# Token mixer of a hybrid trunk: 23 weight pieces rounded by converting transfers, their rests made by an adding transfer

## The chip, the cores and the metric

The kernel runs on one core of one Trainium2 chip. The metric is the device time of one launch in microseconds (us), as the median over runs. Less is better.

## The reference

One layer of a decoder trunk on 16 meta tokens and 512 real tokens of width 1024, in float32: a SwiGLU feed-forward (FFN1), a token mixer, a second SwiGLU feed-forward (FFN2), each added to the residual.

```python
h = h + 0.5 * swiglu(rms_norm(h, g1), ffn1_w_in, ffn1_w_out)
h = h + token_mixer(rms_norm(h, gm), ...)
h = h + 0.5 * swiglu(rms_norm(h, g2), ffn2_w_in, ffn2_w_out)

def token_mixer(h, ...):
    proj = h @ w_in                    # 1024 x (3*512 + 8 + 512 + 2*128 + 2*1024)
    qa, ka, va, fa, qb, kb, vb, ga, gb = split(proj)
    # per-head rms_norm of qa, ka, qb, kb
    log_f = log_sigmoid(fa + forget_bias)
    o_fox = fox_attention(qa, ka, va, log_f)         # 8 heads, causal, with decay
    o_swa = swa_attention(qb, kb, vb, sinks, bias)   # window 128, meta keys, sinks
    y = sigmoid(ga) * (o_fox @ w_branch_fox) + sigmoid(gb) * (o_swa @ w_branch_swa)
    return y @ w_out
```

## The kernel before

**Split products.** TensorE multiplies fp32r numbers, which are rounded float32. To keep float32 accuracy each factor is split into a rounded part and a rest, `x = xH + xL`, `w = wH + wL`, and a product is three matmuls into one PSUM tile: `xH wH`, `xH wL`, `xL wH`. The helper `prod` records all of them, so they stand at L301, L302 and L304 wherever they are used. For the 16 meta tokens `tok_step` uses a packed tile `xm` and two matmuls, L1009 and L1010.

**Pieces of weights.** All weights come in pieces of up to 128 x 1024 float32 (512 KB), in the order of the list `pieces`. A piece of kind "w" goes through three tiles of the pool `wp`: `raw` (loaded by SP's queue, L252), `wh` (rounded by ScalarE, `hi`, L133) and `wl` = `raw - wh` (VectorE, `lo`, L140). Each name has three buffers that are used in turn. Other kinds ("A" to "D") belong to seven-product blocks in the FFNs; some of their loads are added onto a loaded tile by a transfer on POOL's queue (`add`, L211).

**Who drives them.** The user of a piece calls `piece()`. It splits pieces up to `state["ahead"]` = 3 from the one in use (`split_to`) and loads up to 5 from it (`load_to`). The call stands where the first matmul of the piece is recorded, so the loads and splits are recorded ahead of it; a scheduler then orders each engine's recorded instructions. Every engine works through its own order strictly.

**The mixer.** The projection of `w_in` runs in nine chunks of 256 columns, two pieces each: first the first half of `va` (with the 8 forget columns; the pieces are `w0`), then `ka` (k0), `qa` (q0), the other half of `va`, k1, q1, `kv` (keys and values of the window branch), qb0, qb1. Then three gate pieces `wg`, four pieces of the first branch matrix `wbr[0]`, the last gate, and the pieces of `wbr[1]`. Chunks that make tokens go by tiles of 128 tokens (`tok_chunk`), gates and branches by features (`feat_steps`). A chunk of k or q is followed by head norms (`head_norm`: sums of squares on ScalarE, L1061; the power of -1/2 on POOL, `rsq`, L351; scaling on VectorE, L1073), a transpose on TensorE and a split into `qH`, `qL` or `kH`, `kL`. Attention units (scores L1221, exponentials L1181, values L1281) are woven between the chunks.

**Around the start of the mixer** POOL also casts `xm` (L898, L899), loads four small tables (L967 to L970) and fills `v` and `qn` (L1100, L1126).

Of the kernel before, what the change touches and what calls it, by code (L numbers as in the profile page):

```python
# [11 lines left out]
F32 = mybir.dt.float32  # L12
F32R = mybir.dt.float32r
BF16 = mybir.dt.bfloat16
AF = mybir.ActivationFunctionType
ALU = mybir.AluOpType
# [4 lines left out]
P = 128  # L21
# [11 lines left out]
PW = 4 * 264  # L33
# [5 lines left out]
NG = 4  # L39
# [43 lines left out]
def kernel(  # L83
# [22 lines left out]
    V, A, G, PE, SP = nc.vector, nc.scalar, nc.gpsimd, nc.tensor, nc.sync  # L106

    cp = ctx.enter_context(tc.tile_pool(name="const", bufs=1))
    wp = ctx.enter_context(tc.tile_pool(name="wts", bufs=3))
# [6 lines left out]
    def nm(s):  # L116
        nid[0] += 1
        return f"{s}_{nid[0]}"
# [5 lines left out]
    def psum(whole=False):  # L124
        if banks["turn"] is not None:
            whole = banks["turn"] = not banks["turn"]
        tag = "pt" if whole else "ps"
        return pp.tile([P, 512], F32, tag=tag, name=nm(tag))

    def hi(o, i, scale=None):  # L130

        if scale is None:
            return A.copy(o, i)  # L133
        return A.activation(o, i, AF.Identity, scale=scale)
# [13 lines left out]
    pieces = []  # L148
# [26 lines left out]
    ffn_pieces(w1i, w1o, False)  # L175
    for c in (4, 2, 0, 5, 3, 1, 8, 6, 7):
        for k in (0, 4):
            pieces.append(("w", [(wm[c][:, k : k + 4, :], 4, 256)]))
            if c == 4:
                pieces[-1][1].append((wfa[:, k : k + 4, :], 4, 8))  # L180
    pieces += [("w", [(wg[m], 8, 128)]) for m in range(NG - 1)]
    pieces += [("w", [(wbr[0, c], 4, 256)]) for c in range(4)]
    pieces.append(("w", [(wg[NG - 1], 8, 128)]))
    pieces += [("w", [(wbr[1, c], 4, 256)]) for c in range(3)]

# [1 line left out]
    for step in GATES:  # L187
        if step[0] != "sliding":
            m = KD * step[0] + step[1]
# [8 lines left out]
    raws, split = {}, {}  # L198

    xm_place = lambda n: cp.tile([P, KD * P], F32R, tag="xm", name=nm(n))  # L200
    state = {"use": 0, "load": 0, "split": 0}
    shared = {}

    def land(tile_, ap):
# [8 lines left out]
    def load_first(b1, b2, n):  # L213

        raw = wp.tile([P, PW], F32, tag="raw", name=nm("raw"))
        land(raw, b1[:, :n])
        land(raw[:, 128 * n :], b2[:, :n])
        add(raw[:, 128 * n :], b2[:, n:])
        return raw[:, : 256 * n], 2 * n, 128

    def load_others(b1, b2, n):

        w = 128 * n
        fpool = shared["tp"]
        c = fpool.tile([P, PW], F32, tag="rawC", name=nm("rawC"), bufs=2)
        d = fpool.tile([P, 512], F32, tag="rawD", name=nm("rawD"), bufs=2)
        land(c, b1)
        add(c, b2[:, :n])
        land(d, b2[:, n:])

        def sums():
            t = fpool.tile([P, PW], F32, tag="tc", name=nm("tc"), bufs=1)
            V.tensor_tensor(out=t[:, :w], in0=c[:, :w], in1=d[:, :w], op=ALU.add)
            V.tensor_tensor(out=t[:, w : 2 * w], in0=t[:, :w], in1=c[:, w : 2 * w], op=ALU.add)  # L234
            return t[:, : 2 * w], 2 * n, 128

        return sums, (c[:, : 2 * w], 2 * n, 128), (d[:, :w], n, 128)

    def load_to(n):
        while state["load"] < min(n, holds[0] if holds else n, len(pieces)):  # L240
            c = state["load"]
            state["load"] += 1
            kind, *what = pieces[c]
            if kind == "w":
                parts = what[0]
                nk = parts[0][1]
                w = sum(p[2] for p in parts)
                raw = wp.tile([P, PW], F32, tag="raw", name=nm("raw"))
                rv = raw[:, : nk * w].rearrange("p (k c) -> p k c", c=w)
                c0 = 0  # L250
                for ap, _, n_ in parts:
                    SP.dma_start(rv[:, :, c0 : c0 + n_], ap)  # L252
                    c0 += n_
                raws[c] = (raw[:, : nk * w], nk, w)
            elif kind == "A":
                raws[c] = load_first(*what)
            elif kind == "B":
                raws[c], raws[c + 1], raws[c + 2] = load_others(*what)
# [5 lines left out]
    def split_to(n):  # L264
        while state["split"] < min(n, len(pieces)):
            c = state["split"]
            load_to(c + 1)
            state["split"] += 1
            raw = raws.pop(c)
            if callable(raw):  # L270
                with tc.issue_after(shared["lo"]):
                    raw = raw()
            raw, nk, w = raw
            if pieces[c][0] == "D":
                wd = shared["wd"]()
                wh, wl = wd[:, :512], wd[:, 512:1024]
            else:
                wh, wl = (wp.tile([P, PW], F32R, tag=t, name=nm(t)) for t in ("wh", "wl"))
            b = slice(0, nk * w)
            shared["split"] = hi(wh[:, b], raw[:, b]), lo(wl[:, b], raw[:, b], wh[:, b])  # L280
            shared["lo"] = getattr(shared["split"][1], "ins", shared["split"][1])
            split[c] = tuple(t[:, : nk * w].rearrange("p (k c) -> p k c", c=w) for t in (wh, wl))

    def piece(ahead=None, then=None):

        c = state["use"]
        state["use"] += 1
        if then is not None and c in split:
            then(split[c])
            then = None  # L290
        split_to(c + (ahead or state["ahead"]))
        load_to(c + 5)
        if then is not None:
            then(split[c])
        return split.pop(c)

    def prod(outs, sH, sL, first, last, more=False):

# [706 lines left out]
    def tok_step(ps, i, w, k, width):  # L1005
        c0, _ = ttile[i]
        wH, wL = w[k // 4]
        if i == 0:
            PE.matmul(ps[:, :width], xm[:, k], wH[:, k % 4], start=k == 0, stop=False)  # L1009
            PE.matmul(ps[:, :width], xm[:, k], wL[:, k % 4], start=False, stop=k == KD - 1)  # L1010
            return
        prod(
            [(ps[:, :width], wH[:, k % 4], wL[:, k % 4])],
            xH[:, k, c0 : c0 + P],
            xL[:, k, c0 : c0 + P],
            k == 0,
            k == KD - 1,
        )
# [10 lines left out]
    def tok_chunk(alloc, tiles, evac, finish=None):  # L1029

        w, box = [], {}

        def one(i, half):
            if not w:
                alloc()
                w.extend([piece(), piece()])
            if half == 0:
                box[i] = psum()
            for k in range(4 * half, 4 * half + 4):
                tok_step(box[i], i, w, k, 256)  # L1040
            if half:
                box[i] = evac(i, tok_result(box[i], i, 256))
                if i - 1 in box and box[i - 1] is not None:
                    box[i - 1]()

        def end():
            if box[tiles[-1]] is not None:
                box[tiles[-1]]()
            finish()

        st = [lambda i=i, h=h: one(i, h) for i in tiles for h in range(2)]
        if finish is not None:
            st.append(end)
        return st
# [42 lines left out]
    def v_tile():  # L1097

        v = new("v", [P, NB + 1, 512])
        G.memset(v[:, 0].bitcast(F32), 0.0)  # L1100
        return v
# [307 lines left out]
    def feat_steps(wsrc, srcH, srcL, nk, c0, use, cuts=4, w=S, whole=False):  # L1409

        box = {}

        def part(j):
            if j == 0:
                box["w"] = wsrc()
                box["ps"] = psum(whole)
            wH, wL = box["w"]
            for k in range(j * nk // cuts, (j + 1) * nk // cuts):
                prod(
                    [(box["ps"][:, :w], srcH[:, k, c0 : c0 + w], srcL[:, k, c0 : c0 + w])],  # L1420
                    wH[:, k],
                    wL[:, k],
                    k == 0,
                    k == nk - 1,
                )
            if j == cuts - 1:
                use(box["ps"][:, :w])

        return [lambda j=j: part(j) for j in range(cuts)]
# [5 lines left out]
    every, toks = range(NB + 1), range(1, NB + 1)  # L1435
    f0["v"] = v_tile()
    w0 = [piece(), piece()]
    ps0 = [psum() for _ in every]
    for k in range(KD):
        for i in every:  # L1440
            tok_step(ps0[i], i, w0, k, 264)
    V.memset(zf, 0.0)
# [62 lines left out]
    def fox_out(m):  # L1505

        return zA[:, m] if m >= NG - 1 else oF["f"][m // 2][:, S * (m % 2) : S * (m % 2) + S]
# [45 lines left out]
    for m in range(NG - 1):  # L1553
        with after(shared["exp"]):
            A.activation(zA[:, m], zA[:, m], AF.Sigmoid)
        V.tensor_tensor(out=zA[:, m], in0=zA[:, m], in1=fox_out(m), op=ALU.mult)
    stM.close()


    stG = ExitStack()  # L1560
# [165 lines left out]
    for i, step in enumerate(GATES):  # L1726
# [4 lines left out]
        b, m = step  # L1731
# [34 lines left out]
    for hf in range(2):  # L1766
        c = slice(S // 2 * hf, S // 2 * (hf + 1))
# [152 lines left out]
```

## Time and profile before

| | |
|---|---|
| median of 3 runs | 1080.73 us (1080.53 to 1080.74) |
| span of the profiled execution | 1078.4 us |
| the profiled execution's own time beside it | not listed; the median lies 2.3 us above the span |
| TensorE busy, weight loads | 1069.1 us, 1037.1 us |
| VectorE, ScalarE, POOL busy | 891.8, 656.5, 196.2 us |
| mean granted TensorE clock | 0.999 |
| bytes moved by DMA | 173.06 MB |
| the mixer's projections and attention | about 340 to 600 us |

A group line of the profile gives line, engine, operation, tiles and shapes, the count, then busy us and mean ns of one, then idle time just before and what ended it. A timeline line gives the start, the duration, engine, line, operation and tiles, and in brackets the idle time before and its releaser. PE is TensorE's matmul side, PEld its weight loads, DVE is VectorE, ACT is ScalarE, POOL is GpSimd, SP is SyncE.

### The profile page before, as it was taken

How to read it: one execution, taken by the hardware profiler on the slowest of the kernel's cores; microseconds unless marked ns; L12 is line 12 of the kernel's file. 1: busy time of each engine (PE TensorE's matmuls, PEld its weight loads, DVE VectorE, ACT ScalarE, POOL GpSimd, SP SyncE). 2: the span in 40 equal slices, each digit the busy share in tenths (PEclk: the TensorE clock that was granted, in tenths of full speed). 3: DMA queues.
4: the chain of work that ended last, by engine and by line, in shares of the span. 5: the costliest groups of instructions: out<-in, count | busy, mean ns of one | idle time of the engine just before them, and what ended most of it. 6: DMA issues, size and time to landing. Idle time of an engine off the chain costs nothing.

```text
span 1078.4 us, 22338 instructions
## 1 busy us (share of the span) xinstructions
PE 1069.1 (99%) x8587; PEld 1037.1 (96%) x8587; DVE 891.8 (83%) x1718; ACT 656.5 (61%) x1243; POOL 196.2 (18%) x232
## 2 busy tenths in 40 slices
PE   8999999999999999999999999999999999999998
PEld 8999999999999999999887799999999999999998
DVE  7988878888889577788897799788998788887895
ACT  7667456656666455556667866555666466645664
POOL 3011111121124431221200110001122211221120
PEclk9999999999999999999999999999999999999999
DMA  8787778688776423112211765466688877887753
GB/s 280 199 220 161 191 190 197 153 219 213 183 177 171 121 81 118 54 47 81 80 50 50 234 165 149 172 200 197 175 204 164 201 192 179 178 194 193 161 122 104
DMA packets 111723, 173.06 MB, mean 160 GB/s; under 512 B 10800, under 2 KB 58160, under 8 KB 111232
## 3 DMA queue, kind: packets, MB, share of 16 engines
q1 hardware_dynamic: 74032, 122.03, 35.5%
q0 software_dynamic: 28768, 37.83, 22.7%
q10 hardware_dynamic: 8816, 11.77, 3.4%
q8 instruction: 67, 1.10, 0.4%
q14 instruction: 40, 0.33, 0.1%
HBM read 167.37 MB, written 6.32 MB: 161 GB/s over the span
## 4 chain that ended last, share of the span: by engine, by line
PE 92%; DVE 3%; ACT 3%; issue 1%; DMA 0%; POOL 0%; SPq 0%; ACTq 0%; DVEq 0%
PE ps L301 16%; PE ps L304 15%; PE ps L302 15%; PE pt L301 13%; PE pt L302 13%; PE pt L304 13%; ACT t L1181 1%; ACT wh L133 1%; DVE wl L140 1%; PE pt L1221 1%; PE pt L1266 1%; DMA xt<-in_x_dram 0%; PE ps L1388 0%; DVE t L1184 0%; PE ps L1221 0%
## 5 line engine op out<-in xcount | busy, mean ns | idle before, releaser
L301 PE MATMUL ps<-x,wh 128*128 128x256 f32 (+2 forms) x768 | 219.7, 286 | 0.1
L302 PE MATMUL ps<-x,wh 128*128 128x256 f32 (+2 forms) x768 | 218.9, 285 | 0.5 <-DVE x L142 0.4
L304 PE MATMUL ps<-x,wl 128*128 128x256 f32 (+2 forms) x768 | 218.9, 285 | 0.0
L140 DVE TENSOR_TENSOR wl<-raw,wh 128x1024 fp32r<-128x1024 f32 (+3 forms) x125 | 150.0, 1201 | 44.4 <-ACT wh L133 43.1
L133 ACT CAST wh<-raw 128x1024 fp32r<-128x1024 f32 (+3 forms) x125 | 128.5, 1029 | 88.9 <-PE ps L302 58.3
L301 PEld LDWEIGHTS ps<-x,wh 128*128 128x128 f32 x768 | 144.7, 189 | 1.7 <-ACT hT L686 0.3
L302 PEld LDWEIGHTS ps<-x,wh 128*128 128x128 f32 x768 | 144.5, 188 | 1.4 <-DVE x L142 0.9
L304 PEld LDWEIGHTS ps<-x,wl 128*128 128x128 f32 x768 | 144.6, 188 | 0.8
L301 PE MATMUL pt<-x,wh 128*128 128x256 f32 (+2 forms) x424 | 125.3, 297 | 0.2 <-ACT wh L133 0.2
L304 PE MATMUL pt<-x,wl 128*128 128x256 f32 (+2 forms) x424 | 124.5, 294 | 0.0
L302 PE MATMUL pt<-x,wh 128*128 128x256 f32 (+2 forms) x392 | 112.5, 287 | 0.0
L133 ACT CAST wh<-tc 128x1024 fp32r<-128x1024 f32 (+1 forms) x70 | 71.9, 1026 | 64.5 <-DVE tc L234 57.1
L140 DVE TENSOR_TENSOR wl<-tc,wh 128x1024 fp32r<-128x1024 f32 (+1 forms) x70 | 83.5, 1193 | 32.5 <-ACT wh L133 32.2
L301 PE MATMUL ps<-acts,wh 128*128 128x264 f32 (+1 forms) x352 | 100.5, 285 | 0.1
L304 PE MATMUL ps<-acts,wl 128*128 128x264 f32 (+1 forms) x352 | 99.9, 284 | 0.0
L302 PE MATMUL ps<-acts,wh 128*128 128x264 f32 (+1 forms) x352 | 99.5, 283 | 0.0
L140 DVE TENSOR_TENSOR wl<-rawC,wh 128x1024 fp32r<-128x1024 f32 (+1 forms) x70 | 84.2, 1203 | 5.8 <-ACT wh L133 5.5
L133 ACT CAST wh<-rawC 128x1024 fp32r<-128x1024 f32 (+1 forms) x70 | 71.6, 1023 | 22.8 <-PE pt L302 17.8
L301 PEld LDWEIGHTS pt<-x,wh 128*128 128x128 f32 x424 | 79.9, 189 | 2.6 <-ACT wh L133 0.5
L304 PEld LDWEIGHTS pt<-x,wl 128*128 128x128 f32 x424 | 79.7, 188 | 2.1
L302 PEld LDWEIGHTS pt<-x,wh 128*128 128x128 f32 x392 | 73.8, 188 | 0.6
L301 PEld LDWEIGHTS ps<-acts,wh 128*128 128x128 f32 x352 | 66.5, 189 | 0.7 <-DVE h2T L918 0.3
(424 smaller groups left out, 3251.0 us busy)
## 6 DMA issues: line engine op xcount, KB each, us to landing
rawC<-in_w1i_dram SPq DMA_DIRECT2D x20, 512.0 KB, 4.6
raw<-in_w1i_dram SPq DMA_DIRECT2D x40, 256.0 KB, 4.2
raw<-in_w2i_dram SPq DMA_DIRECT2D x40, 256.0 KB, 3.4
rawC<-in_w2i_dram SPq DMA_DIRECT2D x20, 512.0 KB, 4.4
raw<-in_wm_dram SPq DMA_DIRECT2D x18, 512.0 KB, 4.4
raw<-in_wout_dram SPq DMA_DIRECT2D x16, 512.0 KB, 4.0
rawD<-in_w1i_dram SPq DMA_DIRECT2D x20, 256.0 KB, 4.1
raw<-in_w1i_dram POOLq DMA_DIRECT2D x20, 256.0 KB, 5.1
```

The source lines that it names most:

```text
L133: return A.copy(o, i)
L140: return V.tensor_tensor(out=o, in0=i, in1=h, op=ALU.subtract)
L301: PE.matmul(ps, sH, mH, start=first, stop=False, **more)
L302: PE.matmul(ps, sH, mL, start=False, stop=False, **more)
L304: shared["mm"] = PE.matmul(ps, sL, mH, start=False, stop=last, **more)
L1181: shared["exp"] = A.activation(t, t, AF.Exp, bias=nmx, scale=-1.0, accum_out=l[:, j : j + 1])
L1221: PE.matmul(ps[:, :w], q[qx][hb, hp, P * i : P * i + P], k[kx][hb, hp, c0 : c0 + w], start=qx + kx == 0, stop=qx == 1 and not last,)
L1266: PE.transpose(ps[:, c : c + P], ts_[hh][(c // P) % 2][:, c0 : c0 + P], ident)
```

## The change

Pieces get a new kind "m": the eight chunks after the first (16 pieces), three gates and the four pieces of `wbr[0]`, 23 in all. For these no raw tile is loaded by SP. A transfer on POOL's queue reads the float32 weights from DRAM and writes an fp32r tile, converting (`round_by_dma`, L247). ScalarE writes that tile with turned sign into the second tile (`rest_by_dma`, L252). A second transfer on POOL's queue reads the same weights from DRAM again and adds them to it (L253), so that it holds weight minus rounded weight. Both tiles are a `wh` and a `wl` buffer, except that each fourth such piece takes two of the three `raw` buffers. Names of the new tiles begin with `m` (`mwh`, `mwl`, `mraw`). The first chunk, the last gate, `wbr[1]` and everything in the FFNs stay as they were.

While the mixer runs, splits go 2 pieces ahead instead of 3 and loads 4 instead of 5. New calls of `pump()` in the middle of a chunk's or gate's steps record splits up to 2 pieces from the next one. Code behind the new functions moves down by 29 lines and more (L301 becomes L330, L351 L380, L1009 L1038, L1181 L1212).

```diff
             if c == 4:
                 pieces[-1][1].append((wfa[:, k : k + 4, :], 4, 8))
-            pieces.append(("w", [(wm[c][:, k : k + 4, :], 4, 256)]))
+            pieces.append(("w" if c == 4 else "m", [(wm[c][:, k : k + 4, :], 4, 256)]))
...
-    pieces += [("w", [(wg[m], 8, 128)]) for m in range(NG - 1)]
-    pieces += [("w", [(wbr[0, c], 4, 256)]) for c in range(4)]
+    pieces += [("m", [(wg[m], 8, 128)]) for m in range(NG - 1)]
+    pieces += [("m", [(wbr[0, c], 4, 256)]) for c in range(4)]
...
+    def round_by_dma(ap, nk, w):
+        tags = ("raw", "raw") if made[0] % 4 == 3 else ("wh", "wl")
+        made[0] += 1
+        wh, wl = (wp.tile([P, PW], F32R, tag=t, name=nm("m" + t)) for t in tags)
+        wh, wl = (t[:, : nk * w].rearrange("p (k c) -> p k c", c=w) for t in (wh, wl))
+        G.dma_start(wh, ap)
+        return ap, wh, wl
+
+    def rest_by_dma(ap, wh, wl):
+        A.activation(wl, wh.bitcast(F32), AF.Copy, scale=-1.0)
+        G.dma_start(wl, ap, accum_op=ALU.add)
+        return wh, wl
...
     def load_to(n):
+            if pieces[c][0] == "m" and not state["mix"]:
+                return
...
+            if kind == "m":
+                raws[c] = round_by_dma(*what[0][0])
...
     def split_to(n):
+            if pieces[c][0] == "m":
+                split[c] = rest_by_dma(*raw)
+                continue
...
     def piece(ahead=None, then=None):
-        load_to(c + 5)
+        load_to(c + state["room"])
...
+    def pump():
+        split_to(state["use"] + 2)
...
     def tok_chunk(...):            # in one(i, half)
+            if half and i == tiles[1]:
+                pump()
...
     def feat_steps(...):           # in part(j)
+            elif j == 1:
+                pump()
...
     w0 = [piece(), piece()]
+    state.update(mix=True, room=4, ahead=2)
+    load_to(state["use"] + 2)
     ps0 = [psum() for _ in every]
     for k in range(KD):
+        if k == 4:
+            pump()
...
     stM.close()
+    state.update(room=5, ahead=3)
```

In the engines' orders, POOL at the start of the mixer, before (tables, fills, the power of the mixer's norm, then head norms):

```order
L970 DMA snk<-in_sinks_dram 128x8
L1100 MEMSET v_4896 128x512
L1126 MEMSET qn_5105 128x256
L1100 MEMSET v_5430 128x512
L351 TENSOR_TENSOR r_4890<-r_4890,nhalf 128x5
L351 TENSOR_TENSOR hss_5108<-hss_5108,nhalf 16x4
```

The same place after the change; `mwh_4898` and `mwl_4899` are the first piece of the k chunk, `mwh_4901` and `mwl_4902` its second, `mwh_5067` and `mwl_5068` the first of q:

```order
L999 DMA snk<-in_sinks_dram 128x8
L253 DMA mwl_4899<-in_wm_dram 128x1024
L1131 MEMSET v_4892 128x512
L1157 MEMSET qn_5098 128x256
L247 DMA mwh_4901<-in_wm_dram 128x1024
L1131 MEMSET v_5423 128x512
L253 DMA mwl_4902<-in_wm_dram 128x1024
L247 DMA mwh_5067<-in_wm_dram 128x1024
L380 TENSOR_TENSOR r_4886<-r_4886,nhalf 128x5
L253 DMA mwl_5068<-in_wm_dram 128x1024
```

Rounding and adding transfers of the k and q pieces now stand between the fills and ahead of the norm's power.

TensorE where the k chunk meets its second piece, before (`wh_4902`, `wl_4903` the first piece, `wh_4908`, `wl_4909` the second; tile of the meta tokens):

```order
L1010 MATMUL pt_5085<-wl_4903,xm_4312 128x256
L1009 MATMUL pt_5085<-wh_4908,xm_4312 128x256
L1010 MATMUL pt_5085<-wl_4909,xm_4312 128x256
L1009 MATMUL pt_5085<-wh_4908,xm_4312 128x256
L1010 MATMUL pt_5085<-wl_4909,xm_4312 128x256
```

And after:

```order
L1039 MATMUL pt_5078<-mwl_4899,xm_4312 128x256
L1038 MATMUL pt_5078<-mwh_4901,xm_4312 128x256
L330 MATMUL ps_5106<-mwh_4898,x_4304 128x256
L331 MATMUL ps_5106<-mwl_4899,x_4304 128x256
L333 MATMUL ps_5106<-mwh_4898,x_4308 128x256
L1039 MATMUL pt_5078<-mwl_4902,xm_4312 128x256
```

Three matmuls of the next token tile with the first piece moved ahead of the first one that reads the second piece's rest.

POOL at the v chunk after the change (before, these are head-norm steps alone); `5075`, `5076` the chunk's first piece, `5241`, `5242` its second:

```order
L380 TENSOR_TENSOR hss_5201<-hss_5201,nhalf 128x4
L247 DMA mwh_5075<-in_wm_dram 128x1024
L247 DMA mwh_5241<-in_wm_dram 128x1024
L380 TENSOR_TENSOR hss_5234<-hss_5234,nhalf 128x4
L253 DMA mwl_5076<-in_wm_dram 128x1024
L380 TENSOR_TENSOR hss_5276<-hss_5276,nhalf 128x4
L253 DMA mwl_5242<-in_wm_dram 128x1024
```

Four transfers moved in between four head-norm steps.

ScalarE ahead of the window branch's first query tile, before:

```order
L133 CAST wh_6310<-raw_6020 128x1024
L1094 COPY hsq_6297<-ps_6290 64x256
L1025 COPY hsq_6339<-pt_6322 16x256
L133 CAST pH_6353<-ps_6352 128x512
L133 CAST pH_6362<-pt_6361 128x512
L1061 ACTIVATE hsq_6344<-hsq_6339 16x128
L133 CAST pH_6371<-ps_6370 128x128
L134 ACTIVATE qH_6015<-ps_6390,gq 128x512
```

And after, where `mwh_6297` and `mwl_6298` are the second piece of qb0:

```order
L1054 COPY hsq_6322<-pt_6305 16x256
L133 CAST pH_6336<-ps_6335 128x512
L1092 ACTIVATE hsq_6327<-hsq_6322 16x128
L133 CAST pH_6345<-pt_6344 128x512
L133 CAST pH_6354<-ps_6353 128x128
L252 ACTIVATE mwl_6298<-mwh_6297 128x1024
L134 ACTIVATE qH_6004<-ps_6373,gq 128x512
```

The cast of that piece stood seven rows ahead of `qH`; its sign-turned copy stands right ahead of it.

More of the change, by code (lines that the diff above doesn't have):

```diff
@@ L200 @@
     xm_place = lambda n: cp.tile([P, KD * P], F32R, tag="xm", name=nm(n))
-    state = {"use": 0, "load": 0, "split": 0}
+    state = {"use": 0, "load": 0, "split": 0, "room": 5, "mix": False}
     shared = {}
@@ L237, in load_others @@
         return sums, (c[:, : 2 * w], 2 * n, 128), (d[:, :w], n, 128)
+    made = [0]
+    def round_by_dma(ap, nk, w):
[9 more added lines that the diff above has]
+        return wh, wl
     def load_to(n):
@@ L241, in load_to @@
             c = state["load"]
+            if pieces[c][0] == "m" and not state["mix"]:
+                return
             state["load"] += 1
             kind, *what = pieces[c]
-            if kind == "w":
+            if kind == "m":
+                raws[c] = round_by_dma(*what[0][0])
+            elif kind == "w":
                 parts = what[0]
@@ L266, in split_to @@
             c = state["split"]
+            if pieces[c][0] == "m" and not state["mix"]:
+                return
             load_to(c + 1)
```

## The prediction

> **What bounds the kernel now.** I read the page first: busy shares, then the chain.
>
> ```profile
> span 1078.4 us, 22338 instructions
> PE 1069.1 (99%) x8587; PEld 1037.1 (96%) x8587; DVE 891.8 (83%) x1718; ACT 656.5 (61%) x1243; POOL 196.2 (18%) x232
> q1 hardware_dynamic: 74032, 122.03, 35.5%
> q0 software_dynamic: 28768, 37.83, 22.7%
> PE 92%; DVE 3%; ACT 3%; issue 1%; DMA 0%; POOL 0%; SPq 0%; ACTq 0%; DVEq 0%
> ```
>
> TensorE is busy 99% of the span and holds 92% of the chain that ended last. Work taken from VectorE (DVE) can only shorten the 3% of the chain that is DVE's. The 23 changed pieces are used from 376 us (the k chunk's rows below) to the end of the mixer near 600, so the stretches of time around that part come next (columns: stretch, its length, busy us of PE, PEld, DVE, ACT, POOL with counts, clock, DMA share, GB/s).
>
> ```profile
> 360.00:380.00 20.00, 20.00 (x168) 20.00 (x167) 9.10 (x21) 7.85 (x13) 7.52 (x12) 1.00 0.39 111
> 380.00:400.00 20.00, 20.00 (x172) 19.87 (x171) 16.43 (x46) 11.29 (x21) 6.66 (x7) 1.00 0.24 80
> 340.00:600.00 260.00, 257.84 (x1990) 236.56 (x1989) 205.47 (x564) 155.67 (x362) 53.16 (x70) 1.00 0.25 78
> ```
>
> In 340 to 600 us PE has 2.16 us of idle time in 260, the clock is granted in full, and the DMA engines are 25% busy. There is room on ScalarE (ACT), POOL and the DMA engines, and very little to win on PE. From 360 to 400, where the first changed pieces are used, PE has no idle time at all: any lateness there is added to the span.
>
> **What the change removes.** The groups by shape, and the places where the split stands on the chain:
>
> ```profile
> L140 DVE TENSOR_TENSOR wl<-raw,wh 128x1024 fp32r<-128x1024 f32 x33 | 40.7, 1233 | 6.9 <-ACT wh L133 6.8
> 425.66 1.13 DVE wl L140
> 491.72 1.13 DVE wl L140
> 508.17 1.23 DVE wl L140
> ```
>
> 23 subtractions of 1.233 us leave DVE, 28.4 us. That is 14% of its 205.47 busy us here, but only the three rows of the chain, 1.13 + 1.13 + 1.23 = 3.5 us, can come straight off the end. Some of it goes back to whatever was second (PE's own stream), so I take 2.0, with 0 and 3.5 as ends. The 23 loads on SP's queue also go; nothing else waits in that queue here, so this is worth 0.
>
> **What it adds.** On ACT, 23 sign-turned copies replace 23 casts of the same shape. No such copy with a scale stands in this part, so the cast prices it:
>
> ```profile
> L133 ACT CAST wh<-raw 128x1024 fp32r<-128x1024 f32 x33 | 34.7, 1050 | 20.9 <-PE pt L304 9.2 <-PE ps L302 4.1 <-PE pt L302 3.3
> ```
>
> So 1.05 for 1.05: ACT's sum does not move; only the places do. On POOL 46 transfers are issued, two for each piece. The rows of transfers that POOL's queue carries now, and of the plain load that goes:
>
> ```profile
> L211 POOL DMA_DIRECT2D raw<-in_wg_dram x6: 851/856/940, 598.6 to 645.1; - x6
> DMA to landing us min/median/max: 3.6/4.7/8.2
> raw<-in_wm_dram SPq DMA_DIRECT2D x18, 512.0 KB, 4.4
> raw<-in_wg_dram POOLq DMA_DIRECT2D x6, 256.0 KB, 4.6
> h2T<-h1d POOLq DMA_DIRECT2D x1, 1536.0 KB, 8.8
> h2T<-h1d POOLq DMA_DIRECT2D x1, 512.0 KB, 4.4
> ```
>
> Issue: 46 x 0.856 = 39.4 us of POOL in about 260, on top of 53: no bound, but POOL works in order, and its head-norm steps (L351) now queue behind transfers that wait for ACT. The landing line is that of L211, whose transfers add onto their destination.
>
> Length of the rounding transfer (512 KB, converting; no row shows one): at best a plain one, 4.4; at worst as costly for each byte as queue q0, which is mostly adding transfers and takes 22.7% for 37.83 MB against q1's 35.5% for 122.03, so 2.06 times as much. From 512 to 1536 KB the plain transfer grows by 4.4, so 2.2 for each 512 KB; twice that gives 4.4 + 2.2 = 6.6. I take 5.0, nearer the plain row, since the engines are mostly idle here.
>
> Length of the adding transfer (512 KB): the fastest of 256 KB took 3.6; the second half adds 1.1 as plain bytes, so 4.7; from the median 4.6 with doubled bytes, 4.6 + 2.2 = 6.8. I take 5.6, about midway.
>
> Before, a piece followed its buffer by cast + subtraction, 1.05 + 1.23 = 2.3 us, since its load was done early into a buffer of its own. Now load, copy and addition follow the release of the buffer that the matmuls read: 5.0 + 1.05 + 5.6 = 11.7 us. This is the heart of the forecast: the time from release to use must cover 11.7 us instead of 2.3.
>
> The Trainium skill (DMA: Bandwidth & Descriptors, section "Anatomy of one DMA — SWDGE (gpsimd) path") fits such a transfer as 2.0 us plus its bytes over 436e3, estimated as 3.2 us for 512 KB; both transfers and the copy would then be 7.5 us. The trace differs: the plain 512 KB through POOL's queue took 4.4. By the Trainium skill's figure the first loss below would be nil; the sum goes by the rows.
>
> **Where the longer way shows. First, the k chunk at 376 us.**
>
> ```profile
> 368.59 0.28 PE L1009 MATMUL pt<-wh,xm 128*128 128x264 f32 x1
> 368.79 1.05 ACT L133 CAST wh<-raw 128x1024 fp32r<-128x1024 f32 x1 [4.42 <-PE pt L304]
> 369.63 0.53 POOL L1100 MEMSET v<- 128x512 f32 x1
> 375.39 1.18 PE L981 MATMUL ps<-ones,sqacc 128*128 128x2 f32 x10
> 377.45 0.28 PE L1009 MATMUL pt<-wh,xm 128*128 128x256 f32 x1
> 377.93 0.28 PE L1009 MATMUL pt<-wh,xm 128*128 128x256 f32 x1
> ```
>
> The chunk's first piece uses a buffer that FFN1 leaves before the v chunk begins, and comes in time. Its second piece needs the buffer of the v chunk's first piece, which PE leaves at 368.75 (the cast at 368.79 waits for just that). In POOL's order its rounding stands behind the first piece's addition and two fills, the second of which ends before the fill at 369.63: it goes at 369.7 and lands at 374.7; the copy, with ACT idle, ends at 375.8; the addition lands at 375.9 + 5.6 = 381.5. PE, which starts the chunk at 376.4, reaches the piece's rest after the first five matmuls of the second piece's kind and three put ahead, at about 377.9. Loss 3.6. Ends: 369.7 + 4.4 + 1.1 + 4.7 = 379.9, loss 2.0; 369.7 + 6.6 + 1.1 + 6.8 = 384.2, loss 6.3.
>
> **Second, the v chunk at 403 us.**
>
> ```profile
> 389.72 1.01 POOL L351 TENSOR_TENSOR hss<-hss,nhalf 128x4 f32<-128x4 f32 x1 [0.21 <-DVE hss L1063]
> 394.05 1.01 POOL L351 TENSOR_TENSOR hss<-hss,nhalf 128x4 f32<-128x4 f32 x1 [1.14 <-DVE hss L1063]
> 403.67 0.28 PE L301 MATMUL pt<-wh,x 128*128 128x256 f32 x1
> ```
>
> Both its roundings stand on POOL behind the head-norm step that ends at 390.73, so they go at 390.7 and 391.6; the second lands at 396.6, its copy ends at 397.9 (another copy stands ahead), and its addition stands behind the first one's and a head-norm step: 398.9 + 5.6 = 404.5. PE wants it eight matmuls into the chunk, at 403.67. Loss 0.9; ends 0 and 3.6 (lengths 6.6 and 6.8).
>
> **Third, a copy ahead of a query's rounding at 469 us.**
>
> ```profile
> 460.54 1.01 POOL L351 TENSOR_TENSOR hss<-hss,nhalf 128x4 f32<-128x4 f32 x1 [2.59 <-DVE hss L1063]
> 469.17 0.69 ACT L134 ACTIVATE qH<-ps,gq 128x512 fp32r<-128x512 f32 x1 [1.87 <-PE ps L1139]
> 469.91 0.18 PEld L1221 LDWEIGHTS ps<-kH,qH 64*128 64x128 f32 x1 [0.17 <-ACT qH L134]
> ```
>
> In the new order the copy for the second qb0 piece stands on ACT just ahead of this qH. Two roundings leave POOL at 461.6 and 462.6; the second lands between 467.0 (4.4) and 469.2 (6.6), and the copy ends between 468.1 and 470.2, against 469.17. PE already waits for qH, so a delay passes on: 0 to 1.1; I take 0.7, since the two share the engines.
>
> **Fourth, copies among the exponentials of the late pieces.**
>
> ```profile
> 507.08 1.05 ACT L133 CAST wh<-raw 128x1024 fp32r<-128x1024 f32 x1 [0.73 <-PE pt L304]
> 512.77 0.74 ACT L1181 ACTIVATE t<-t,nmx 128x528 f32<-128x528 f32 x1
> 561.79 1.06 ACT L133 CAST wh<-raw 128x1024 fp32r<-128x1024 f32 x1 [1.57 <-PE ps L302]
> 564.75 0.42 ACT L1181 ACTIVATE t<-t,nmx 128x145 f32<-128x145 f32 x1 [1.91 <-DVE nmx L1375]
> ```
>
> A buffer freed at 507.05 gives a rounding that lands at 512.4, and its copy stands ahead of the exponentials of 512.77: 0.7 late, of which I take 0.6. A buffer freed at 561.8 lands at 566.8, and its copy stands among the four exponentials that begin at 564.75: up to 2.0, I take 0.9. Ends of both together 0 and 4. At the other copies the release lies 10 us or more ahead of the use, and other matmuls cover them: 0.
>
> **The sum.** 3.6 + 0.9 + 0.7 + 1.5 - 2.0 = +4.7 us. The profiled execution's span of 1078.4 becomes 1083.1. The median of the runs, 1080.73, lies 2.3 above that span, so the forecast is 1080.7 + 4.7 = 1085.4 us, slower by 0.4%. With the losses at their low ends and the gain at 3.5 it is 2.0 - 3.5, about 1079.2; with the high ends, 6.3 + 3.6 + 1.1 + 4.0 and no gain, 1095.7.
>
> **The rivals.**
> - The transfers are quick: PE doesn't wait at 377.9, and DVE's relief wins. It decides at 377.9 - 369.7 - 1.1 = 7.1 us for both transfers together. For it: the low traffic (25%) and the fastest adding transfer of 3.6, which twice over is 7.2. Against it: the plain 512 KB row alone takes 4.4. Losses of some 0.5, gain 3: 1078.2 us. Chance 0.24. The figure of the Trainium skill (DMA: Bandwidth & Descriptors, the same section), 3.2 for each, would lead to this case.
> - Nothing to see: losses of about 2, as the low ends have them, against a gain of 2, since PE is the bound and the pieces are made ahead: 1080.7 us. For it: PE's 2.16 us of idle time in 260, so DVE is hardly waited for. Chance 0.14.
> - POOL's order becomes the bound: an addition waits for its copy, the copy for its rounding, and each holds the head-norm steps behind it on POOL and the casts behind it on ACT, for which every chunk's evacuations wait. With transfers of 8 us (the longest adding one took 8.2) a piece takes 17 us and the k, q and v chunks, some 13 us apart, each lose 4 to 5: 1095 to 1105, say 1098 us. For it: 46 waits in two in-order engines. Against: 25% traffic. Chance 0.15.
> - The transfer doesn't round: the rest is then zero and the time is that of my forecast; it changes the output, not the time.
>
> **How the numbers follow.** My forecast (1085.4; its own range 1082 to 1091) has 0.47. About 0.2%, 2.2 us, is what a measurement can tell from no change. Slower: 0.47 + 0.15 = 0.62; same 0.14; faster 0.24. The range runs from 1077.5 (gain 3.5, losses of 0.3) to 1095.7 (all high ends): it leaves out a part of the fast and most of the POOL case.
>
> **What would show it.** A PE wait of 2 to 6 us for a DMA near 377 us, ended by the second piece's addition, and one of about 1 near 404; landing times of the rounding and adding transfers near 5.0 and 5.6; ACT's copies at 1.05; DVE down by 28 us with the matmuls' total unchanged; the two FFNs as before. Wrong if the two transfers take under 7.1 us together, or if waits stand at every chunk.

## The result and the profile after

The changed kernel takes 1097.14 us (median of 5 runs, 1094.3 to 1097.74) against 1080.73: 1.0143 times as long, 95% interval 1.0132 to 1.0155. It is slower by 16 us. Forecast were 1085.4 us and a range up to 1095.7, so the direction was right and the size was a third of what came. The profiled execution, which the profile below shows, took 1095.26 us itself, 1.9 less than the median; its span is 15.0 us longer than that of the kernel before.

The page of the profiled execution (its span; busy times; the queues of transfers; shares of the chain by engine):

```profile
span 1093.4 us, 22360 instructions
PE 1074.7 (98%) x8587; PEld 1041.6 (95%) x8587; DVE 867.6 (79%) x1695; ACT 656.7 (60%) x1243; POOL 230.0 (21%) x278
q0 software_dynamic: 35392, 61.95, 32.5%
q1 hardware_dynamic: 70720, 109.97, 31.8%
PE 84%; DVE 5%; issue 4%; ACT 4%; DMA 2%; POOL 1%; ACTq 0%; POOLq 0%; DVEq 0%
```

VectorE lost 24 us (28 were forecast), ScalarE nothing, POOL gained 34 (39 forecast). But PE's share of the chain fell from 92% to 84%. The stretches, with the columns of before:

```profile
380.00:400.00 20.00, 16.48 (x128) 16.48 (x129) 9.68 (x36) 9.66 (x18) 8.01 (x9) 0.91 0.44 95
400.00:420.00 20.00, 17.84 (x140) 17.19 (x139) 8.74 (x21) 6.31 (x12) 8.26 (x10) 0.91 0.70 175
340.00:600.00 260.00, 248.07 (x1914) 228.42 (x1914) 170.26 (x514) 144.24 (x336) 86.45 (x115) 0.99 0.52 122
```

In 340 to 600 us PE has 11.9 us of idle time where it had 2.2, and from 380 to 420 the granted clock (TensorE's share of its full clock, third figure from the end of a row) is 0.91 where it was 1.00: two losses, of which only the first was in the forecast. PE's waits, largest first (us in total, times, longest; the 1.5 of line L374 stands at the program's start, in both kernels):

```profile
PE pt L1039 <- DMA mwl<-in_wm_dram: 5.0, 1, 5.0
PE pt L1170 <- DVE qn L1104: 2.2, 1, 2.2
PE ps L374 <- POOL ident masks.py:199: 1.5, 1, 1.5
PE ps L1170 <- DVE qn L1104: 1.2, 1, 1.2
PE ps L1252 <- DVE pL L140: 0.8, 1, 0.8
```

In the kernel before, no wait of PE between 340 and 620 us is over 0.4; that for a scaled `qn` is this one:

```profile
PE ps L301 <- DVE qn L1073: 0.4, 1, 0.4
```

The first wait of the changed kernel is the k chunk's for the adding transfer. L1170 are the transposes behind the head norms of a k or q chunk: PE waits there for the scaled `qn`. How long the transfers took (twelve of the sixteen pieces of the chunks, rounding and adding, then the gates' rounding), with the landing lines of all of L247 (rounding) and L253 (adding), in that order:

```profile
mwh<-in_wm_dram POOLq DMA_DIRECT2D x12, 512.0 KB, 5.1
mwl<-in_wm_dram POOLq DMA_DIRECT2D x12, 512.0 KB, 6.2
mwh<-in_wg_dram POOLq DMA_DIRECT2D x3, 512.0 KB, 3.6
DMA to landing us min/median/max: 3.6/4.8/8.8
DMA to landing us min/median/max: 5.1/6.0/9.2
```

So 5.0 and 5.6 were near: the medians are 4.8 and 6.0. The lengths were not the mistake.

**Where PE falls behind.** I matched PE's matmuls of both traces in order and took the difference of their starts, rounded to 0.1 us. The columns are the time of the same matmul in the kernel before: the k chunk's start, its end, the q chunk's end, and on through the chunks; 505.8 and later is the part of gates and branches. With three pairs of buffers PE's order differs so much near 424.7 and 449.0 that other matmuls there give up to 31 and 36. The further rows are experiments, told below.

| kernel | 376.6 | 388.6 | 400.6 | 424.7 | 449.0 | 473.3 | 505.8 | 603.2 |
|---|---|---|---|---|---|---|---|---|
| changed | 0.4 | 7.0 | 10.9 | 12.9 | 13.8 | 14.9 | 14.6 | 14.6 |
| copy reads a constant | 0.4 | 5.7 | 5.6 | 5.6 | 5.4 | 5.2 | 5.2 | 5.1 |
| no adding transfer | 0.1 | 0.1 | 2.2 | 3.7 | 7.2 | 8.3 | 8.1 | 8.5 |
| k chunk of the old kind | 1.9 | 1.9 | 8.3 | 9.0 | 10.7 | 13.5 | 15.7 | 15.4 |
| three pairs of buffers | 0.4 | 5.9 | 13.0 | 22.4 | 25.4 | 42.5 | 47.4 | 54.4 |

In the changed kernel 6.6 us are lost in the k chunk and 7.9 in the chunks behind it. Behind 475 us nothing more is lost, though seven pieces of the new kind are still to come. Of the 7.9, 3.9 come in the q chunk (the wait of 2.2 us above and the lower clock behind it, told below) and 1.2 at the other wait for `qn`; the rest is in waits of 0.8 us or less.

### The profile page after: what moved, and what is told of

Its sections match the earlier page's. It is cut to its first block, busy times and chain, and to the rows that moved or that the text cites. A ratio compares the mean times of both kernels' runs of the same rounds, so it can differ in the third digit from the quotient of the medians.

```text
span 1093.4 us, 22360 instructions
## 1 busy us (share of the span) xinstructions
PE 1074.7 (98%) x8587; PEld 1041.6 (95%) x8587; DVE 867.6 (79%) x1695; ACT 656.7 (60%) x1243; POOL 230.0 (21%) x278
## 4 chain that ended last, share of the span: by engine, by line
PE 84%; DVE 5%; issue 4%; ACT 4%; DMA 2%; POOL 1%; ACTq 0%; POOLq 0%; DVEq 0%
PE ps L330 14%; PE ps L333 14%; PE ps L331 14%; PE pt L330 12%; PE pt L331 12%; PE pt L333 12%; DMA mwh<-in_wm_dram 1%; DVE wl L140 1%; ACT wh L133 1%; PE ps L374 1%; DMA h1d<-hT 1%; DMA mwl<-in_wm_dram 1%; PE ps L1419 0%; POOL hss L380 0%; DVE acts L459 0%
## 5 line engine op out<-in xcount | busy, mean ns | idle before, releaser
L331 PE MATMUL ps<-x,wh 128*128 128x256 f32 (+1 forms) x752 | 213.0, 283 | 0.5 <-DVE x L142 0.4
L330 PE MATMUL ps<-x,wh 128*128 128x256 f32 (+1 forms) x752 | 212.9, 283 | 0.2
L333 PE MATMUL ps<-x,wl 128*128 128x256 f32 (+1 forms) x752 | 212.7, 283 | 0.0
L140 DVE TENSOR_TENSOR wl<-raw,wh 128x1024 fp32r<-128x1024 f32 (+3 forms) x102 | 122.3, 1200 | 38.9 <-ACT wh L133 37.5
L133 ACT CAST wh<-raw 128x1024 fp32r<-128x1024 f32 (+3 forms) x102 | 104.3, 1025 | 74.0 <-PE ps L331 56.8
L330 PEld LDWEIGHTS ps<-x,wh 128*128 128x128 f32 x752 | 141.8, 189 | 0.9 <-ACT hT L715 0.3
L331 PEld LDWEIGHTS ps<-x,wh 128*128 128x128 f32 x752 | 141.5, 188 | 1.0 <-DVE x L142 0.9
L333 PEld LDWEIGHTS ps<-x,wl 128*128 128x128 f32 x752 | 141.9, 189 | 0.2
L330 PE MATMUL pt<-x,wh 128*128 128x256 f32 (+2 forms) x416 | 122.1, 294 | 0.3 <-ACT wh L133 0.3
L333 PE MATMUL pt<-x,wl 128*128 128x256 f32 (+2 forms) x416 | 121.5, 293 | 0.0
L331 PE MATMUL pt<-x,wh 128*128 128x256 f32 (+2 forms) x384 | 109.3, 285 | 0.0
L330 PE MATMUL ps<-acts,wh 128*128 128x264 f32 (+1 forms) x352 | 100.5, 285 | 0.1
L330 PEld LDWEIGHTS pt<-x,wh 128*128 128x128 f32 x416 | 78.5, 189 | 2.2 <-ACT wh L133 0.5
L331 PEld LDWEIGHTS pt<-x,wh 128*128 128x128 f32 x384 | 72.3, 188 | 0.3
L330 PEld LDWEIGHTS ps<-acts,wh 128*128 128x128 f32 x352 | 66.4, 189 | 0.7 <-DVE h2T L947 0.3
```

The costliest lines, as they stand in the source:

```text
L140: return V.tensor_tensor(out=o, in0=i, in1=h, op=ALU.subtract)
L330: PE.matmul(ps, sH, mH, start=first, stop=False, **more)
L331: PE.matmul(ps, sH, mL, start=False, stop=False, **more)
L333: shared["mm"] = PE.matmul(ps, sL, mH, start=False, stop=last, **more)
```

## What a held head norm looks like

At 401 us, in the changed kernel's timeline (start, duration, engine, line, operation; in brackets the idle time and what ended it):

```profile
398.18 1.06 POOL L380 TENSOR_TENSOR hss<-hss,nhalf 128x4 f32<-128x4 f32 x1
401.24 1.06 ACT L252 ACTIVATE mwl<-mwh 128x1024 fp32r<-128x1024 f32 x1 [3.94 <-DMA mwh<-in_wm_dram]
402.20 0.37 ACT L1092 ACTIVATE hsq<-ps 128x256 f32<-128x256 f32 x1
402.60 0.42 DVE L1093 TENSOR_REDUCE hss<-hsq 128x4 f32<-128x256 f32 x1 [4.20 <-ACT hsq L1092]
403.20 0.48 DVE L1104 SCALAR_TENSOR_TENSOR qn<-pt,r,hss 128x256 f32<-128x256 f32 x1
403.44 1.14 POOL L380 TENSOR_TENSOR hss<-hss,nhalf 128x4 f32<-128x4 f32 x1
403.73 0.48 PE L1170 MATMUL pt<-ident,qn 128*128 128x128 f32 x1 [2.16 <-DVE qn L1104]
```

ScalarE stands 3.94 us in front of a sign-turned copy whose rounding transfer has not landed. The squares of a head norm (`hsq`) are next in its order and start in the moment the copy ends. VectorE has waited 4.20 us for them. The `qn` for which PE waits 2.16 us is not made from these squares, though: their power begins on POOL only at 403.44, when that `qn` (403.20) is under way. It is the `qn` of the token tile before, whose power ended on POOL at 399.24. It stood behind the reduction of the new squares in VectorE's order. So one copy held two engines: the squares on ScalarE, and by them a finished tile's scaling on VectorE. The piece that was copied is not used before 413 us: it was in no hurry. ScalarE's waits for rounding transfers, in the changed kernel:

```profile
ACT mwl L252 <- DMA mwh<-in_wm_dram: 26.6, 9, 7.8
```

In the kernel before, a cast on ScalarE waited for a buffer to be released, and the data was there; now each copy waits for a transfer that starts only at that release.

## The experiments

My theory after the result ("buffer to use") was that rounding, copy and addition follow one another behind the release of a buffer, some 13 us, and that the engines that wait for them hold other work. Medians of the kernel before beside these runs were 1080.3 to 1081.8 us.

**Is it the new order alone?** All pieces old, the shorter distances and the `pump` calls kept:

```diff
-            pieces.append(("w" if c == 4 else "m", ...
+            pieces.append(("w", ...                      # the gates and wbr[0] too
```

> All pieces stay of the old kind (SP load, ScalarE cast, VectorE subtraction); only the distances (2 and 4 pieces ahead in the mixer) and the new pump calls stay. Theory 'buffer to use' (each changed piece needs rounding, copy and adding transfer one after the other, behind the release of its buffer, and the engines that wait for it work in order): no loss here, 1079.5 to 1082.5 us. Rival 'order' (the shorter distances and the new places of the calls cost the time): 1088 us or more.

1080.72 us, ratio 1.0003 (0.9993 to 1.0012). The order and the distances cost nothing.

**The late pieces alone** (the 16 chunk pieces old; gates and `wbr[0]` new):

> The 16 pieces of the nine chunks stay of the old kind, the 7 late ones (three gates, four of the first branch matrix) are rounded and completed by transfers. Theory 'buffer to use': the changed kernel lost nothing behind 490 us, so 1079.5 to 1082 us. Rival 'relief': the 7 subtractions taken from VectorE stand between exponentials and shorten the late part by 1 to 3 us: 1078 to 1079.5 us. Rival 'traffic' (POOL's transfers slow the rest wherever they are): 1084 us or more.

1080.5 us, ratio 1.0005 (0.9995 to 1.0014). Neither loss nor gain. Its stretch of late work, then the same of the kernel before:

```profile
520.00:600.00 80.00, 79.57 (x494) 65.04 (x493) 59.19 (x191) 54.56 (x137) 11.11 (x15) 1.00 0.41 100
520.00:600.00 80.00, 79.56 (x492) 65.01 (x491) 66.01 (x196) 54.99 (x137) 4.25 (x5) 1.00 0.16 54
```

VectorE is relieved of 6.8 us in 80 and PE does the same work in the same time. The relief is worth nothing here, where the forecast had 2.0 us for all 23 pieces; and 2.6 times the DMA share (0.41 for 0.16) costs nothing either.

**Halves of the change.** Rounding by transfer, the rest by VectorE from a raw tile:

```diff
+        SP.dma_start(raw, ap)
         G.dma_start(wh, ap)
...
-        A.activation(wl, wh, AF.Copy, scale=-1.0); G.dma_start(wl, ap, accum_op=ALU.add)
+        lo(wl, raw, wh)
```

> The rounded part comes by the converting transfer, the rest by VectorE from a raw tile that SP loads early, as before; no copy on ScalarE, no adding transfer, no pair of raw tiles. Theory 'buffer to use': the way from release to use is one transfer of 4 to 6 us and 1.2 us instead of 13; the k chunk's wait is 0 to 1 us; but VectorE now waits for transfers ahead of the head norms where ScalarE did, 2 to 5 us in all: 1083 to 1087 us. Rival 'adding transfer' (its doubled traffic alone is the cause): 1080 to 1082 us. Rival 'rounding transfer' (late whatever follows it): 1092 us or more.

1102.8 us, ratio 1.0208 (1.0184 to 1.0233). And rounding by ScalarE, only the addition by transfer:

```diff
-        G.dma_start(wh, ap)
+        SP.dma_start(raw, ap)
...
+        hi(wh, raw)
         A.activation(wl, wh, AF.Copy, scale=-1.0); G.dma_start(wl, ap, accum_op=ALU.add)
```

> The raw tile is loaded by SP and rounded by ScalarE as before; ScalarE then makes the sign-turned copy, and the adding transfer completes it (24 us more on ScalarE, no converting transfer). Theory 'buffer to use': 2.1 us of ScalarE plus 5.5 to 6 us of transfer behind the release, so the k chunk's rest lands near 377 us, in time, and ScalarE waits for no transfer: 1080 to 1084 us. Rival 'adding transfer' (POOL's order and the doubled traffic are the cause): 1090 us or more.

1126.21 us, ratio 1.0431 (1.0411 to 1.0451). Both halves are slower than the whole, against my expectation. They differ from it in one thing that I had taken for small: they need the `raw` tiles, so no piece takes its pair from them, and three pairs go round where the changed kernel has more.

**Three pairs, nothing else changed:**

```diff
-        tags = ("raw", "raw") if made[0] % 4 == 3 else ("wh", "wl")
+        tags = ("wh", "wl")
```

> As the changed kernel, but every changed piece takes a wh and wl buffer; none takes a pair of raw buffers, so there are three pairs in turn and not four. Theory 'buffer to use': each chunk's second piece then follows the release of a buffer shortly ahead of its use, with 13 us of rounding, copy and addition between; the kernel that rounds on ScalarE and only adds by transfer, also with three pairs and some 8 us, took 1126: this one 1145 to 1175 us. Rival 'order on ScalarE' (the number of buffers doesn't matter, only the held head norms do): 1094 to 1100 us.

1136.44 us, ratio 1.0511 (1.0490 to 1.0532): short of the 1145 expected, but 39 us slower than the changed kernel. PE's largest waits here:

```profile
PE pt L330 <- DMA mwl<-in_wm_dram: 9.7, 2, 5.7
PE pt L1038 <- DMA mwl<-in_wm_dram: 7.7, 3, 3.9
PE ps L330 <- DMA mwl<-in_wm_dram: 6.8, 2, 4.3
PE ps L1038 <- DMA mwl<-in_wm_dram: 5.0, 1, 5.0
```

With three pairs a chunk's second piece gets its buffer when the chunk before ends. The old way (cast and subtraction, 2.3 us) fits behind that; the half with rounding and subtraction loses 22 us, the half with cast, copy and addition 46, the full chain 55. What the fourth pair hid is most of this; the k chunk's second piece is one that doesn't have it.

**The k chunk of the old kind:**

```diff
-            pieces.append(("w" if c == 4 else "m", ...
+            pieces.append(("w" if c in (4, 2) else "m", ...
```

> As the changed kernel, but the two pieces of the first k chunk stay of the old kind (so the raw pair goes to the second pieces of other chunks: v, q1, qb0, the second gate). Theory 'buffer to use': the 5.0 us wait at 378 us and the clock dip behind it, 6.6 us together, go, the rest stays: 1089 to 1092 us. Rival 'moves on' (the next chunk that lacks an own pair waits instead): 1094 us or more.

1094.93 us, ratio 1.0124 (1.0107 to 1.0140). The rival held: the wait moved on. The k chunk loses nothing (1.9 and 1.9 in the table; the 1.9 stand there before the mixer), and the q chunk loses 6.4 instead, since its second piece now has no pair of its own:

```profile
396.44 0.39 PE L330 MATMUL ps<-mwh,x 128*128 128x256 f32 x1 [2.51 <-DMA mwh<-in_wm_dram]
403.25 0.39 PE L331 MATMUL ps<-mwl,x 128*128 128x256 f32 x1 [1.35 <-DMA mwl<-in_wm_dram]
```

**The copy on another engine.**

```diff
-        A.activation(wl, wh.bitcast(F32), AF.Copy, scale=-1.0)
+        V.tensor_scalar(out=wl, in0=wh.bitcast(F32), scalar1=-1.0, scalar2=None, op0=ALU.mult)
```

> The sign-turned copy is made by VectorE instead of ScalarE; everything else as in the changed kernel. Theory 'order on ScalarE' (copies that wait for a rounding transfer hold the squares of the head norms behind them on ScalarE, 8 us in all behind the first wait): those 8 us go or halve, the first wait of 5.0 us stays: 1087 to 1091 us. Rival 'any engine' (VectorE then holds the rest of the same head norms): 1093 to 1100 us.

1095.58 us, ratio 1.0141 (1.0108 to 1.0174): as the changed kernel. With the same line on POOL (`G.tensor_scalar`):

> The sign-turned copy is made by POOL, just ahead of the adding transfer that POOL issues. Theory 'order on ScalarE': ScalarE never waits for a transfer, POOL waited there anyway; the first wait grows by the longer copy (1 to 2 us), the other 8 us shrink to 3 to 5: 1091 to 1095 us. Rival 'any engine' (the head norms' steps on POOL are held longer): 1098 us or more.

1111.93 us, ratio 1.0281 (1.0250 to 1.0311). With VectorE (a copy took 0.69 us there, 1.06 on ScalarE) the loss is not smaller, which speaks for "any engine": each of the three carries a step of the head norms, and a copy that waits there can hold one. POOL says less of that, since its copy took longer:

```profile
L252 POOL TENSOR_SCALAR mwl<-mwh x18: 2765/2779/3158, 367.8 to 598.2; 128x1024 fp32r<-128x1024 f32 x18
```

At 2.8 us for a copy the way from release to use grows too, and both losses with it: 13.0 us in the k chunk, 15.0 behind. There PE waits 13.4 us for adding transfers and only 1.0 for `qn`, so this run doesn't show a held head norm.

**Taking the waits apart.** Let the copy read a constant, so that it and the addition no longer follow the rounding (the rest is then no rest; transfers, copies and buffers are the same in number and size):

```diff
-        A.activation(wl, wh.bitcast(F32), AF.Copy, scale=-1.0)
+        A.activation(wl, ident (eight times), AF.Copy, scale=-1.0)
```

> As the changed kernel, but ScalarE's copy reads a constant tile of the same size instead of the rounded piece (so the rest is wrong); number and size of the transfers, copies and buffers are unchanged, but the copy and the adding transfer no longer follow the rounding transfer. Theory 'one behind the other': rounding and adding run side by side, some 7 to 8 us behind the release, ScalarE waits for no transfer: 1080.5 to 1084 us. Rival 'load' (the number of transfers on POOL's queue and their traffic cost the time): 1092 us or more.

1087.99 us, ratio 1.0065 (1.0050 to 1.0080), between the two expectations. The table shows what that mixes: behind the k chunk the loss is gone altogether (5.7, then 5.6 to 5.1), though every transfer is still there. In the k chunk 5.3 us stay. So traffic and the number of issues on POOL cost nothing in the chunks behind the k chunk. The whole is 8.4 us longer by its span all the same: 3.0 of them come behind 603 us, where the code is that of the kernel before, and their cause was not looked for.

The opposite experiment: the copy waits as before, the adding transfer is left out.

```diff
         A.activation(wl, wh.bitcast(F32), AF.Copy, scale=-1.0)
-        G.dma_start(wl, ap, accum_op=ALU.add)
```

> As the changed kernel, but the adding transfer is left out (the rest is the sign-turned copy alone, so wrong); the copy still waits for the rounding transfer. Theory 'held head norms': the first wait (5.0 us and the clock dip) goes, since the copy ends near 377.7 us; the losses behind it, 8 us, come from copies that wait on ScalarE ahead of head norms and stay: 1086 to 1090 us. Rival 'late rests' (all losses come from the adding transfer's end or its traffic): 1081 to 1083 us.

1089.75 us, ratio 1.0081 (1.0059 to 1.0102). The k chunk loses nothing, and 8.4 us are lost behind it, though no rest can be late for PE by an addition now. The waits of PE and ScalarE here (lines stand one higher than in the changed kernel):

```profile
PE pt L1169 <- DVE qn L1103: 1.9, 1, 1.9
PE ps L1251 <- DVE pL L140: 1.6, 1, 1.6
PE ps L1169 <- DVE qn L1103: 1.2, 1, 1.2
ACT mwl L252 <- DMA mwh<-in_wm_dram: 20.0, 9, 4.2
```

These two experiments divide the loss: the first keeps the k chunk's and drops the rest, the second drops the k chunk's and keeps the rest. What they share with the changed kernel tells the cause: behind the k chunk time is lost in the kernels whose copy waits for its rounding transfer, and in the other it isn't. That the work held by it is head norms is read from the waits for `qn`, for some 5 of the 7.9 us.

**Who is held.** Squares of the head norms on VectorE, so that ScalarE holds none, and the same edit in the kernel before as a control:

```diff
-        A.activation(sq, ps, AF.Square)
+        V.tensor_copy(sq, ps); V.tensor_tensor(out=sq, in0=sq, in1=sq, op=ALU.mult)
```

> As the changed kernel, but the squares of the head norms are made by VectorE (a copy and a product, some 0.9 us each time) instead of ScalarE, so that a copy waiting on ScalarE holds no head norm. Theory 'held head norms': the first wait stays, of the 8 us behind it 4 or more go: 1087 to 1092 us, if the control (the kernel before with the same edit) stays within 1 us of 1080.7. Rival 'late rests': 1095 us or more.

> Control: the kernel before with the squares of the head norms on VectorE. Both theories: 1080 to 1083 us; what it loses is taken off the kernel with the same edit.

1095.6 and 1088.07 us. The control is not within 1 us: the edit itself costs 7.8, so the expectation for the first can't be read as it stands. With the edit in both, the change costs 7.5 us instead of 16.4; behind the k chunk PE falls back 6.3 us with the change and 6.4 without. That fits held head norms, but VectorE is loaded so heavily by the edit that its relief by the change may count here too. I lean on the two experiments above, not on this pair.

**The clock.** The k chunk loses more than its wait: 6.6 for 5.0 us, and with the constant copy 5.3 for 2.5. The profile shows a lower clock there. The kernel with the constant copy, columns as above, the clock third from the end:

```profile
378.00:380.00 2.00, 0.16 (x2) 0.00 (x0) 1.16 (x7) 0.51 (x1) 1.34 (x2) 0.86 1.03 291
380.00:382.00 2.00, 1.34 (x6) 1.37 (x7) 0.00 (x0) 0.00 (x0) 0.00 (x0) 0.50 1.00 201
382.00:384.00 2.00, 2.00 (x11) 2.00 (x10) 0.57 (x2) 1.44 (x4) 0.00 (x0) 0.50 0.69 135
384.00:386.00 2.00, 2.00 (x11) 2.00 (x11) 1.94 (x7) 1.24 (x4) 0.00 (x0) 0.50 0.01 2
386.00:388.00 2.00, 2.00 (x18) 2.00 (x18) 1.38 (x7) 1.97 (x4) 1.04 (x1) 0.93 0.00 0
388.00:390.00 2.00, 2.00 (x20) 2.00 (x19) 0.98 (x5) 1.97 (x3) 0.40 (x1) 1.00 0.00 0
```

PE waits 2.5 us, till 380.7, and then runs at half the clock for more than 5: 11 matmuls in 2 us instead of 20 (a dip of the clock, below). To tell this from the late transfer I filled the wait with matmuls of no use, 42 in the changed kernel, 20 in that with the constant copy:

```diff
+                for _ in range(42):        # 20
+                    PE.matmul(spare[:, :256], xm[:, 0], w[0][0][:, 0], start=True, stop=True)
                 PE.matmul(ps[:, :width], xm[:, k], wL[:, k % 4], ...)   # the one that waited
```

> As the changed kernel, with 42 matmuls of no use (4.9 us at 0.117) put ahead of the one in the k chunk that waits 5.0 us. Theory 'clock dip' (the half clock behind a wait costs more time than the wait): the granted clock stays at 1.00 behind 383 us and the lag of TensorE in the k chunk falls from 6.6 to about 5.7 us; the whole about 1 us faster than the changed kernel. Rival 'no dip' (the lag is the late transfer alone): the lag stays at 6.5 us or grows.

> As the kernel whose copy reads a constant tile (its rest is wrong), with 20 matmuls of no use (2.3 us) ahead of the one that waited 2.5 us. Theory 'clock dip': clock 1.00 throughout, lag in the k chunk 2.8 us instead of 5.3, 1085 to 1086 us instead of 1088. Rival 'no dip': lag 5.3 us or more, 1088 us.

With the constant copy: 1085.61 us, 2.4 less than without, as expected; the k chunk loses 3.2 us instead of 5.3 (2.8 expected); the clock stays at 1.00 (here the stretch that showed 0.50), and the matmul that waited starts 0.2 us later than before at 380.84, so nothing came sooner but the clock:

```profile
382.00:384.00 2.00, 2.00 (x20) 2.00 (x19) 0.87 (x4) 1.95 (x4) 0.00 (x0) 1.00 0.64 123
380.84 0.36 PE L1044 MATMUL pt<-mwl,xm 128*128 128x256 f32 x1 [0.58 <-ACT v L134]
```

In the changed kernel the dip of the k chunk went too, and the chunk lost 6.2 us instead of 6.6 (5.7 expected). But the next wait for `qn` grew from 2.2 to 3.9 us, and the whole took 1099.57 us instead of about 1 us less than the changed kernel. In its profile PE is 15.5 us behind at 603 and 18.7 at the end, where the changed kernel has 14.6 and 15.0; so most of the excess lies behind the mixer. That expectation failed; why the next head norm came later, and the loss at the end, were not tried.

## Why the prediction was wrong

- **Direction and first place.** Right: the k chunk's second piece comes late for the reason given. Its rounding went at 370.6 (369.7 forecast) and took 5.9 us (5.0), the addition 5.5 (5.6); the wait was 5.0 us for the 3.6 forecast, within the ends of 2.0 and 6.3. The clock's dip behind it, 1.6 us, was in no term. Of the 14.5 us lost, this place has 6.6.
- **The step that failed: "At the other copies the release lies 10 us or more ahead of the use, and other matmuls cover them: 0."** The pieces were indeed covered. But I asked only when the piece itself is needed, and not what stands behind its copy in ScalarE's order. The squares of the head norms do, and PE needs them soon. This term was 7.9 us instead of 0, some 1.6 of them a second dip of the clock; the kernel without the adding transfer shows it alone as 8.4, and it vanishes when the copy doesn't wait for its rounding. I had named the mechanism in the POOL rival ("each holds the head-norm steps behind it on POOL and the casts behind it on ACT"), with a chance of 0.15, but tied it to transfers of 8 us. It needs no such length: the medians were 4.8 and 6.0.
- **Second to fourth place.** The v chunk's wait for its addition (0.9) didn't come: PE reached that chunk later, and the addition was there. The loss at `qH` (0.7) didn't come as told: the copy ahead of it ended at 483.2, and ScalarE then waited 0.86 us for PE before `qH`; the 1.2 us lost just there were the other wait for `qn`. The losses among the exponentials (1.5) are not to be seen as a lag: from 473.3 to 603.2 it goes from 14.9 to 14.6.
- **The gain of 2.0** was 0 in the late part (the pieces there alone: ratio 1.0005), and at most 0.6 over the whole (5.7 falling to 5.1 with the constant copy). In the late part PE did the same work in the same time without it: PE's own stream stood right behind VectorE's rows of the chain.
- **The sum.** 6.6 + 7.9 = 14.5 in the trace, and 0.4 of lag before the k chunk, for 4.7 forecast; the span grew by 15.0, the median by 16.4.
- **The Trainium skill's figure** (DMA: Bandwidth & Descriptors, "Anatomy of one DMA — SWDGE (gpsimd) path") gave an estimate of 3.2 us for 512 KB. The gates' rounding transfers took 3.6, those of the chunks 5.1, their additions 6.2: the measurements decide against the quick rival.

## What to carry to other kernels

When a wait is put into an engine's order, price what stands behind it there, not only the result that the waiting instruction makes: a copy that nobody needed for 10 us held a head norm for which TensorE stood idle 2.2. A step that begins only when a buffer is released must be compared, over its whole chain, with the time from release to use; here one more pair of buffers was worth 39 us, and half of the chain with one pair less was worse than all of it. Work taken from an engine at 83% was worth nothing here, where another was at 99%.

## What the runs showed of the hardware

A wait of PE can cost more than its length. After idle times of 2.5 and 5.0 us the granted clock was 0.50 for 5.5 and about 3 us, which cost another 2.8 and 1.6; with the wait filled by idle matmuls the clock stayed at 1.00 and 2.4 us came back. The changed kernel, behind its wait of 5.0 us that ended at 383.5, and behind its wait of 2.2 us that ended at 403.7:

```profile
384.00:386.00 2.00, 2.00 (x11) 2.00 (x11) 0.19 (x1) 0.59 (x2) 0.00 (x0) 0.50 0.05 16
404.00:406.00 2.00, 2.00 (x12) 1.59 (x11) 1.55 (x4) 1.38 (x3) 1.47 (x2) 0.50 0.84 115
```

The length of the dip doesn't follow that of the wait. In the records of the clock both dips of the changed kernel last 3.41 us and that with the constant copy 6.83; all dips of the mixer in the runs told here last one to four times 3.41. Nor does each wait bring one: without the adding transfer, PE's idle time of 1.93 us up to 396.6 left the clock at 1.00, and one of 1.62 up to 438.8 was followed by a dip from 439.5 on.

The Trainium skill (TensorE: Matmul & The Clock Gate, "HAM oscillation — how this bites in real kernels") has the rule that PE should have no gaps above some 3.4 us. Half the clock is what the trace shows; here waits of 2.2 and 2.5 us, shorter than the rule's, were followed by it.
